# Batched matrix-product trace: last row tile loaded in other pieces, row 15 shared between TensorE and VectorE

## The chip, the cores and the metric

The kernel runs on one core of a Trainium2 chip. The metric is the device time of one execution in microseconds (us); each figure is a median of several runs. Before the change the time was 709.94 us (3 runs).

## The reference

```python
def reference(a, b):                        # a, b: (8, 2176, 2176) float32
    prod = np.matmul(a, b)
    return np.diagonal(prod, axis1=1, axis2=2).sum(axis=-1)
```

The trace of a product needs no product: it is the sum over all i, k of a[i, k] * b[k, i]. So the kernel transposes a, multiplies it element by element with b, and adds everything up. All 303 MB of the inputs must be read once.

## The kernel before

For each batch the rows of `a` are loaded as bf16, transposed by TensorE and copied into the tile `at`. The rows of `b` then come in groups of 128 (a "row tile", 17 in a batch, numbered 0 to 16). There are two ways to use one:

- VectorE: one fused multiply-and-reduce of a row tile with its part of `at`. It shows as CUSTOM_DVE_ANT_1, followed by a short read of the accumulator.
- TensorE: the row tile is cut into blocks of 128 columns. Each block is a matmul of a block of `at` with a block of `b`, added into one 128 x 128 tile, `trace_ps`. Only the diagonal of it is wanted; VectorE takes it at the end with a multiply-and-reduce against the identity (the "diagonal reduction" below, CUSTOM_DVE_ANT_0).

A row tile has five column groups: four of 512 columns (4 matmuls each) and a narrow one of 128 columns (1 matmul). In seven of the eight batches VectorE does all rows of `b`. In the last batch some go to TensorE, so that little is left to do when the last bytes arrive:

```python
PE_ROWS = (11, 12, 13, 15)
LAST_PIECES = [(0, 2), (2, 3), (3, 5)]      # column groups of row 16: three DMAs
...
def multiply_on_pe(at, row, v, g0, g1, parts=ROWS):
    for g in range(g0, g1):
        x, y = words_at(at, v, g, g + 1), words_of(row, g, g + 1)
        if g == n_wide:                      # the narrow group: weights from the row
            pe_work.append((row[:, g * WIDE:N], x.rearrange("q r x -> q x r")))
        else:                                # weights from at
            pe_work.extend((x[:, r, :], y[:, r, :]) for r in range(parts))
...
# row 16, the last one
multiply_on_pe(at, row, v0, 0, 1)
late.append((words_at(at, v0, 1, 2), words_of(row, 1, 2)))
half = ROWS // 2
for g in range(2, n_wide):
    multiply_on_pe(at, row, v0, g, g + 1, parts=half)
    late.append((words_at(at, v0, g, g + 1)[:, half:, :], words_of(row, g, g + 1)[:, half:, :]))
multiply_on_pe(at, row, v0, n_wide, len(a_groups))
...
for n, (x, y) in enumerate(pe_work):         # all TensorE work, in this order
    nc.tensor.matmul(trace_ps, x, y, start=(n == 0), stop=(n == len(pe_work) - 1))
...
for x, y in late:                            # VectorE's last reductions, in this order
    multiply_reduce(x, y, late_acc[:, cols:cols + 1]); cols += 1
multiply_reduce(tiles[f32], trace_ps, late_acc[:, cols:cols + 1], out=tiles["diagonal"])
# then: ones x late_acc on TensorE, a short sum on VectorE, the output DMA
```

Of the kernel before, what the change touches and what calls it, by code (L numbers as in the profile page):

```python
# [10 lines left out]
def row_groups(p, rows):  # L11

    groups, at = [], 0
    for m in rows:
        groups.append((at, m))
        at += m * p
    return groups
# [3 lines left out]
def kernel(  # L21
# [20 lines left out]
    a_groups = row_groups(P, even)  # L42
# [2 lines left out]

    UNEVEN = ((0, 80), (80, 119), (119, P))

    PE_ROWS = (11, 12, 13, 15)

    LAST_PIECES = [(0, 2), (2, 3), (3, 5)]  # L50

    const = ctx.enter_context(tc.tile_pool(name="const", bufs=1))
    at_pool = ctx.enter_context(tc.tile_pool(name="at_pool", bufs=1))
# [6 lines left out]
    def joined(groups):  # L60

        loads = []
        for start, m in groups:
            if m == ROWS and loads and loads[-1][1:] == (ROWS, 1):
                loads[-1] = (loads[-1][0], ROWS, DOUBLE)
            else:
                loads.append((start, m, 1))
        return loads
# [3 lines left out]
    def in_order():  # L72

        return tc.issue_after(loaded[-1].ins) if loaded else nullcontext()

    def fetch(t, src, start, m, count, parts=((0, P),)):

        rows = src[start:start + P * m * count, :].rearrange("(g p r) k -> p g r k", g=count, r=m)
        part = t.rearrange("p (g r) k -> p g r k", r=m)
        for lo, hi in parts:  # L80
            with in_order():
                issued = nc.gpsimd.dma_start(out=part[lo:hi], in_=rows[lo:hi])  # L82
            loaded.append(issued)
        return [(start + g * P * m, m, t[:, g * m:(g + 1) * m, :]) for g in range(count)], issued

    def load(src, start, m, count, parts=((0, P),)):
        if m == 1:
            t = single.tile([P, 1, N], bf16, tag="single")
        else:
            t = stage.tile([P, DOUBLE * ROWS, N], bf16, tag="stage")  # L90
        return fetch(t[:, 0:count * m, :], src, start, m, count, parts)

    def load_first(src, start):

        words = stage.tile([P, DOUBLE * ROWS, N], bf16, tag="stage")
        plain = words.bitcast(f32).rearrange("p r k -> p (r k)")[:, :N]
        half = N // 2
        t = single.tile([P, 1, N], bf16, tag="single")
        nc.sync.dma_start(out=plain, in_=src[start:start + P, :])
        nc.scalar.copy(out=t[:, 0, :half], in_=plain[:, :half])  # L100
        nc.vector.tensor_copy(out=t[:, 0, half:], in_=plain[:, half:])  # L101
        return [(start, 1, t)]
# [3 lines left out]
    def constants():  # L106
        identity32 = const.tile([P, P], f32, tag="identity32")
        make_identity(nc, identity32)
        identity16 = const.tile([P, P], bf16, tag="identity16")
        make_identity(nc, identity16)  # L110
        ones = const.tile([P, 1], f32, tag="ones")
        nc.vector.memset(ones, 1.0)
        sums = const.tile([P, BATCH], f32, tag="sums")
        late = const.tile([P, 2 * NT], f32, tag="late")
        diagonal = const.tile([P, P], bf16, tag="diagonal")
        result = const.tile([P, BATCH], f32, tag="result")
        tiles.update(ones=ones, sums=sums, late=late, result=result, diagonal=diagonal)
        tiles[f32], tiles[bf16] = identity32, identity16
# [12 lines left out]
    def multiply_reduce(x, y, acc, out=None):  # L131

        nc.vector.tensor_tensor_reduce(  # L133
            out=x if out is None else out, in0=x, in1=y, scale=1.0, scalar=0.0,
            op0=MUL, op1=ADD, accum_out=acc,
        )
# [4 lines left out]
    n_wide = NT // ROWS  # L141
# [58 lines left out]
    def words_of(row, g0, g1):  # L200

        return row[:, g0 * WIDE:min(g1 * WIDE, N)].rearrange("q (x r) -> q r x", r=ROWS)

    def words_at(at, v, g0, g1):
        return at[:, :, v, g0 * P:min(g1 * P, WORDS)]
# [3 lines left out]
# [4 lines that stand above are left out]
            if g == n_wide:  # L213
                pe_work.append((row[:, g * WIDE:N], x.rearrange("q r x -> q x r")))
            else:
                pe_work.extend((x[:, r, :], y[:, r, :]) for r in range(parts))

    late = []
    ahead = None
    for bi in range(BATCH):  # L220
        last = bi == BATCH - 1
        b_groups = row_groups(P, fine if last else even)


        at = at_pool.tile([P, ROWS, NT, WORDS], bf16, tag="at")
        loads = joined(a_groups)
        if bi == 0:
            loads = loads[-1:] + loads[:-1]
        for start, m, count in loads:
            if not tiles:  # L230
                groups = load_first(a[bi], start)
                ahead, issued = load(a[bi], *loads[1])
                with tc.issue_after(issued.ins):
                    constants()
            elif ahead is not None:
                groups, ahead = ahead, None
            else:
                groups, _ = load(a[bi], start, m, count)
            for start, m, a_t in groups:
                last_transpose = transpose_group(at, a_t, start, m, b_groups)  # L240


        copies_end = last_copy
        acc = tiles["late"] if last else acc_pool.tile([P, NT], f32, tag="acc")
        cols = 0

        def on_dve(v0, rows):

            nonlocal cols
            m = rows.shape[1]  # L250
            with tc.issue_after(copies_end.ins):
                multiply_reduce(
                    at[:, :, v0:v0 + m, :].rearrange("q r v x -> q r (v x)"),
                    rows.rearrange("q s (x r) -> q r (s x)", r=ROWS),
                    acc[:, cols:cols + 1],
                )
            cols += 1

        if not last:
            for start, m, count in joined(b_groups):  # L260
                parts = UNEVEN if bi == BATCH // 2 and m == 1 else ((0, P),)
                groups, _ = load(b[bi], start, m, count, parts)
                for start, m, b_t in groups:
                    on_dve(start // P, b_t)
            nc.vector.reduce_sum(  # L265
                out=tiles["sums"][:, bi:bi + 1], in_=acc[:, :cols], axis=mybir.AxisListType.X
            )
            continue

        used = DOUBLE * ROWS  # L270
        for start, m in b_groups:
            v0 = start // P
            if start < N - P:

                if used + m > DOUBLE * ROWS or m < ROWS and used == ROWS:
                    shared = stage.tile([P, DOUBLE * ROWS, N], bf16, tag="stage")
                    used = 0
                (group,), _ = fetch(shared[:, used:used + m, :], b[bi], start, m, 1)
                used += m
                b_t = group[2]  # L280
                mine = [s for s in range(m) if v0 + s not in PE_ROWS]
                if mine:
                    on_dve(v0 + mine[0], b_t[:, mine[0]:mine[-1] + 1, :])
                for s in range(m):
                    if s not in mine:
                        multiply_on_pe(at, b_t[:, s, :], v0 + s, 0, len(a_groups))
                continue
            b_t = single.tile([P, 1, N], bf16, tag="single")
            row = b_t[:, 0, :]
            for g0, g1 in LAST_PIECES:  # L290
                lo, hi = g0 * WIDE, min(g1 * WIDE, N)
                with in_order():
                    loaded.append(nc.gpsimd.dma_start(  # L293
                        out=row[:, lo:hi], in_=b[bi, start:start + P, lo:hi]
                    ))
            multiply_on_pe(at, row, v0, 0, 1)
            late.append((words_at(at, v0, 1, 2), words_of(row, 1, 2)))
            half = ROWS // 2
            for g in range(2, n_wide):
                multiply_on_pe(at, row, v0, g, g + 1, parts=half)  # L300
                late.append((words_at(at, v0, g, g + 1)[:, half:, :], words_of(row, g, g + 1)[:, half:, :]))
            multiply_on_pe(at, row, v0, n_wide, len(a_groups))


    trace_ps = psum_small.tile([P, P], f32, tag="trace")
# [57 lines left out]
```

## Time and profile before

| what | value | how to read it |
|---|---|---|
| time | 709.94 us | median of 3 runs |
| span of the profile | 707.9 us | the recorded part of one run |
| busiest engine | VectorE, 56% | no compute engine is the bound over the whole |
| DMA engines | 90% busy or more in 39 of 40 slices | the loads are the bound until they end |
| row 15 of the last batch lets TensorE start | 701.58 us | all that follows is "the tail" |
| diagonal reduction starts | 705.12 us | 3.54 us after that |

In the timeline a line has the start, the duration, the engine (PE is TensorE, PEld its weight loads, DVE is VectorE), the line of the kernel, the operation, output<-inputs, the shape and the count. In brackets it has the idle time before, and what ended it. `shared` holds the rows of the last batch up to row 15, `b_t` is row 16. The prediction shows the lines of the kernel before.

### The profile page before, as it was taken

How to read it: one execution, taken by the hardware profiler on the slowest of the kernel's cores; microseconds unless marked ns; L12 is line 12 of the kernel's file. 1: busy time of each engine (PE TensorE's matmuls, PEld its weight loads, DVE VectorE, ACT ScalarE, POOL GpSimd, SP SyncE). 2: the span in 40 equal slices, each digit the busy share in tenths (PEclk: the TensorE clock that was granted, in tenths of full speed). 3: DMA queues.
4: the chain of work that ended last, by engine and by line, in shares of the span. 5: the costliest groups of instructions: out<-in, count | busy, mean ns of one | idle time of the engine just before them, and what ended most of it. 6: DMA issues, size and time to landing. Idle time of an engine off the chain costs nothing.

```text
span 707.9 us, 3257 instructions
## 1 busy us (share of the span) xinstructions
PE 194.4 (27%) x1322; PEld 180.3 (25%) x1322; DVE 399.6 (56%) x200; ACT 196.5 (28%) x211; POOL 36.0 (5%) x63
## 2 busy tenths in 40 slices
PE   1542005420055100651005500056000670005605
PEld 0432005420054100551005500056000660005605
DVE  0222995138942389424893338933489334883396
ACT  2443005430064200642006510066100660006700
POOL 1000000000010000000001000000000000000100
PEclk9977557675577755776557765577655775557855
DMA  9999999999999999999999999999999999999997
GB/s 220 220 219 213 210 222 220 216 209 216 224 219 209 219 218 220 211 217 219 217 212 216 219 219 212 217 219 216 214 215 219 217 214 215 219 218 216 212 215 153
DMA packets 11681, 152.28 MB, mean 215 GB/s; under 512 B 914, under 2 KB 1170, under 8 KB 3346
## 3 DMA queue, kind: packets, MB, share of 16 engines
q0 software_dynamic: 11520, 150.97, 100.3%
q1 hardware_dynamic: 146, 1.11, 0.4%
q8 instruction: 10, 0.16, 0.1%
q14 instruction: 5, 0.04, 0.0%
HBM read 303.04 MB, written 0.00 MB: 428 GB/s over the span
## 4 chain that ended last, share of the span: by engine, by line
DMA 58%; DVE 24%; another core or an unknown queue 8%; issue 6%; PE 2%; ACT 1%; POOL 1%; DVEq 0%; POOLq 0%
DMA t<-in_b_dram 41%; DVE at L133 23%; DMA t<-in_a_dram 13%; DMA shared<-in_b_dram 4%; PE ps L167 1%; ACT at L128 1%; DVE at L126 1%; PE trace_ps L308 0%; POOL t L82 0%; PE ps L188 0%; POOL shared L82 0%; DVE acc L133 0%; POOL identity masks.py:199 0%; DVEq L133 0%
## 5 line engine op out<-in xcount | busy, mean ns | idle before, releaser
L128 ACT COPY at<-ps 128x1024 bf16<-128x1024 bf16 x208 | 194.1, 1051 | 471.4 <-PE ps L167 471.4
L133 DVE CUSTOM_DVE_ANT_1 at<-at,t 128x8704 bf16<-128x8704 bf16 (+1 forms) x35 | 273.6, 7862 | 81.2 <-DMA t<-in_b_dram 81.2
L167 PE MATMUL ps<-identity,t 128*128 128x128 f32 x1071 | 174.2, 328 | 481.8 <-DMA t<-in_a_dram 471.1
L167 PEld LDWEIGHTS ps<-identity,t 128*128 128x128 f32 x1071 | 162.0, 213 | 491.1 <-issue 463.0
L126 DVE COPY at<-ps 128x1024 bf16<-128x1024 bf16 (+2 forms) x104 | 94.2, 909 | 214.8 <-PE ps L167 197.7
L82 POOL DMA_DIRECT2D t<-in_a_dram x23 | 15.3, 669 | 344.3 <-DVE acc L133 199.9
L133 DVE CUSTOM_DVE_ANT_1 at<-at,shared 128x8704 bf16<-128x8704 bf16 (+2 forms) x4 | 27.8, 6955 | 1.9 <-DMA shared<-in_b_dram 1.9
L82 POOL DMA_DIRECT2D t<-in_b_dram x23 | 14.8, 646 | 237.7 <-PE ps L188 118.5
L188 PE MATMUL ps<-identity,t 128*128 128x128 bf16 x170 | 16.4, 219 | 5.1 <-DVE at L126 4.7
L188 PEld LDWEIGHTS <-t 128*128 128x128 bf16 x170 | 13.0, 100 | 8.5 <-issue 8.2
L308 PEld LDWEIGHTS <-at 128*128 128x128 bf16 x72 | 8.3, 124 | 24.7 <-issue 24.5
L308 PE MATMUL trace_ps<-shared,at 128*128 128x128 bf16 x64 | 8.1, 294 | 23.9 <-DMA shared<-in_b_dram 23.9
L82 POOL DMA_DIRECT2D shared<-in_b_dram x6 | 3.2, 537 | 55.1 <-PE ps L188 35.8
L101 DVE CAST t<-words 128x1088 bf16<-128x1088 f32 x1 | 0.7, 727 | 4.8 <-DMA words<-in_a_dram 4.8
L133 DVE DVE_READ_ACCUMULATOR2_ANT acc<- 128x1 f32 x35 | 2.9, 82 | 0.0
L133 DVE CUSTOM_DVE_ANT_1 at<-at,b_t 128x256 bf16<-128x256 bf16 (+1 forms) x3 | 1.5, 515 | 1.7 <-DMA b_t<-in_b_dram 1.7
L100 ACT CAST t<-words 128x1088 bf16<-128x1088 f32 x1 | 1.1, 1099 | 3.7 <-DMA words<-in_a_dram 3.7
L293 POOL DMA_DIRECT2D b_t<-in_b_dram x3 | 1.6, 567 | 0.0
L308 PE MATMUL trace_ps<-at,shared 128*128 128x128 bf16 x4 | 1.6, 396 | 0.0
L100 ACT ACT_TABLE_LOAD x1 | 1.3, 1283 | 0.7 <-PEq L347 0.7
L265 DVE TENSOR_REDUCE sums<-acc 128x1 f32<-128x5 f32 x7 | 1.1, 158 | 0.2
L308 PE MATMUL trace_ps<-b_t,at 128*128 128x128 bf16 x8 | 1.1, 296 | 0.0
(18 smaller groups left out, 4.3 us busy)
## 6 DMA issues: line engine op xcount, KB each, us to landing
t<-in_a_dram POOLq DMA_DIRECT2D x16, 4352.0 KB, 45.6
t<-in_b_dram POOLq DMA_DIRECT2D x14, 4352.0 KB, 52.2
shared<-in_b_dram POOLq DMA_DIRECT2D x3, 2176.0 KB, 43.0
t<-in_a_dram POOLq DMA_DIRECT2D x7, 544.0 KB, 47.4
t<-in_b_dram POOLq DMA_DIRECT2D x6, 544.0 KB, 54.8
words<-in_a_dram SPq DMA_DIRECT2D x1, 1088.0 KB, 4.9
shared<-in_b_dram POOLq DMA_DIRECT2D x1, 1088.0 KB, 26.1
shared<-in_b_dram POOLq DMA_DIRECT2D x2, 544.0 KB, 29.3
```

The source lines that it names most:

```text
L82: issued = nc.gpsimd.dma_start(out=part[lo:hi], in_=rows[lo:hi])
L100: nc.scalar.copy(out=t[:, 0, :half], in_=plain[:, :half])
L101: nc.vector.tensor_copy(out=t[:, 0, half:], in_=plain[:, half:])
L126: last_copy = nc.vector.tensor_copy(out=dst, in_=src)
L128: nc.scalar.copy(out=dst, in_=src)
L133: nc.vector.tensor_tensor_reduce(out=x if out is None else out, in0=x, in1=y, scale=1.0, scalar=0.0, op0=MUL, op1=ADD, accum_out=acc,)
L167: nc.tensor.transpose(ps[:, n * m + r, :], words[:, r, c0:c0 + step * (P - 1) + 1:step], tiles[f32],)
L188: last_transpose = nc.tensor.transpose(ps16[:, n, r, :], a_t[:, r, c0:c0 + P], tiles[bf16],)
L265: nc.vector.reduce_sum(out=tiles["sums"][:, bi:bi + 1], in_=acc[:, :cols], axis=mybir.AxisListType.X)
L293: loaded.append(nc.gpsimd.dma_start(out=row[:, lo:hi], in_=b[bi, start:start + P, lo:hi]))
L308: nc.tensor.matmul(trace_ps, x, y, start=(n == 0), stop=(n == len(pe_work) - 1),)
```

## The change

The intent is to shorten what TensorE has still to do after the last load. Row 15 is no longer all TensorE's: VectorE gets 1152 of its 2176 columns. The last row comes from the right, the wide piece with the narrow group first, so that two short matmuls and a short reduction are left for the last piece.

```diff
-    PE_ROWS = (11, 12, 13, 15)
-    LAST_PIECES = [(0, 2), (2, 3), (3, 5)]
+    PE_ROWS = (11, 12, 13)
+    SHARED_ROW = 15
+    LAST_PIECES = [(2, 5), (1, 2), (0, 1)]
 ...
+                if v0 == SHARED_ROW:
+                    row = b_t[:, 0, :]
+                    multiply_on_pe(at, row, v0, 0, 2)
+                    late.append((words_at(at, v0, 2, 5), words_of(row, 2, 5)))
+                    continue
 ...
-            multiply_on_pe(at, row, v0, 0, 1)
-            late.append((words_at(at, v0, 1, 2), words_of(row, 1, 2)))
+            multiply_on_pe(at, row, v0, n_wide - 1, len(a_groups))
+            late.append((words_at(at, v0, 2, n_wide - 1), words_of(row, 2, n_wide - 1)))
             half = ROWS // 2
-            for g in range(2, n_wide):
+            for g in (1, 0):
                 multiply_on_pe(at, row, v0, g, g + 1, parts=half)
                 late.append((words_at(at, v0, g, g + 1)[:, half:, :], words_of(row, g, g + 1)[:, half:, :]))
-            multiply_on_pe(at, row, v0, n_wide, len(a_groups))
```

## The prediction

> **What bounds the kernel now.** I read the page of the profile first, then the chain that ended last, then the timeline of its last microseconds. On the page, the engines' shares and the slices give the answer for most of the span:
>
> ```profile
> PE 194.4 (27%) x1322; PEld 180.3 (25%) x1322; DVE 399.6 (56%) x200; ACT 196.5 (28%) x211; POOL 36.0 (5%) x63
> ...
> DMA  9999999999999999999999999999999999999997
> ...
> HBM read 303.04 MB, written 0.00 MB: 428 GB/s over the span
> ```
>
> No engine is busy for more than 56%, while the 16 DMA engines are full in 39 of 40 slices; only the last slice shows a 7. So the loads bind until they end, and the change moves none of their bytes. What it can change is what happens around and after the last loads. The chain says how the end hangs together:
>
> ```profile
> 671.22 30.32 DMA shared<-in_b_dram
> 701.54 0.04 issue
> 701.58 3.39 PE trace_ps L308 x26
> 704.97 0.03 issue
> ...
> 705.12 0.29 DVE diagonal L133
> ```
>
> Row 15 of the last batch (a "shared" tile) lands at 701.54. From there on the chain is not DMA but 26 matmuls in a row: 17 of row 15 and 9 of the last row (b_t). Then VectorE reduces the diagonal of the TensorE product, and the final sum and the output follow. The timeline shows both engines in that stretch:
>
> ```profile
> 701.58 2.01 PE L308 MATMUL trace_ps<-shared,at 128*128 128x128 bf16 x16 [0.91 <-DMA shared<-in_b_dram]
> ...
> 702.82 0.69 DVE L133 CUSTOM_DVE_ANT_1 at<-at,b_t 128x512 bf16<-128x512 bf16 x1 [1.34 <-DMA b_t<-in_b_dram]
> ...
> 703.47 0.43 DVE L133 CUSTOM_DVE_ANT_1 at<-at,b_t 128x256 bf16<-128x256 bf16 x1
> 703.63 1.11 PE L308 MATMUL trace_ps<-b_t,at 128*128 128x128 bf16 x8
> ...
> 704.26 0.43 DVE L133 CUSTOM_DVE_ANT_1 at<-at,b_t 128x256 bf16<-128x256 bf16 x1 [0.36 <-DMA b_t<-in_b_dram]
> 704.45 0.13 PEld L308 LDWEIGHTS <-b_t 128*128 128x128 bf16 x1
> 704.56 0.40 PE L308 MATMUL trace_ps<-at,b_t 128*128 128x128 bf16 x1
> 704.62 0.09 DVE L133 DVE_READ_ACCUMULATOR2_ANT late<- 128x1 f32 x1
> 705.12 0.29 DVE L133 CUSTOM_DVE_ANT_0 diagonal<-identity,trace_ps 128x128 bf16<-128x128 f32 x1 [0.42 <-PE trace_ps L308]
> ```
>
> Three readings. TensorE begins the last row at 703.63, some 0.8 us after its first piece let VectorE go (702.82): it is behind by the work of row 15. VectorE in the same time waits: 1.34 us for the first piece and 0.36 us for the last. The last piece released VectorE at 704.26, so by the same 0.04 us of lag that row 15 shows (701.54 to 701.58) it landed at about 704.22; a count over 704.3 to 708.0 shows no DMA share at all. TensorE reaches that piece (the seventh of the nine matmuls) only at 703.63 + 6 x 0.116 = 704.33, so it never waits for it. The bound after the loads is thus the tail of a backlog, and a short one: the lag is about 0.1 us.
>
> **What the Trainium skill says.** "TensorE: Matmul & The Clock Gate", section "Single matmul latency", gives (219+N)/1.2 ns for the cold clock: for N = 128 that is 289 ns. The granted clock is 0.50 from 680 us on, and the matmuls take 292 to 297 ns: it agrees. Its section "LDWEIGHTS" gives P/1.2, 107 ns; this trace has 123 to 127 ns, and the pitch of the pairs is (704.56 - 703.63)/8 = 0.116 us. I use the trace's pitch. "VectorE: DVE Perf Modes", section "The TRN2 errata", tells of a fixed cost per instruction beside the elements, some 150 cycles measured at 0.96 GHz. Here 512 elements take 693 ns and 256 take 426 ns, so 1.04 ns each and 0.16 us fixed, which is about 154 cycles: it agrees. "DMA: Bandwidth & Descriptors", section "Queues, rings and completion order", has each DMA engine consume its descriptors in ring order, without a guarantee that writes complete in it. The releases at 702.82 and 704.26 follow the order of issue, and I assume that for the new pieces.
>
> **The change, part by part.** The bytes are the same, as are the number of DMAs (three for the last row) and their queue, so I keep 704.22 for the last landing. The last row takes 704.22 - 701.54 = 2.68 us for 2176 columns, or 1.23 ns a column. As a check, the old first piece of 1024 columns gives 702.80 by this, and VectorE was let go at 702.82. The new landings (estimates): 1152 columns at 702.96, 512 more at 703.59, the last 512 at 704.22.
>
> TensorE. Of row 15 it keeps column groups 0 and 1, 2 x 4 = 8 matmuls of 17; 9 go. They start at 701.58 and end 8 x 0.116 later, at 702.51, so TensorE is idle when the first piece lands. That piece is 5 matmuls (one group of 4 and the narrow one of 128 columns): from 703.00 on, issued by 703.58. The second is 2 matmuls, from 703.63 to 703.86. The third is 2 matmuls, from 704.26: the second starts at 704.38 and takes 0.29, so the product is done at 704.67. Before it was done at 704.97. The 0.30 us has three parts: the backlog of 0.07 to 0.1 (704.33 against 704.26); one matmul fewer in the last piece, 0.116; and a last matmul of 0.29 in place of 0.40, as the narrow one, whose weights come from the row itself, is no longer last.
>
> VectorE. It gains one reduction of 1152 elements: 0.16 + 1152 x 1.04 ns = 1.36 us. It was free from 701.48 (the accumulator read after row 14), so this runs from 701.58 to 702.94, to about 703.0 with the read of its sum: within the wait of 1.34 us shown above. Then 512 elements of the first piece, 703.0 to 703.65 (the old one took 0.65 to the next start); 256 of the second, to 704.05; 256 of the third from 704.26, with the read done at 704.71 as before. No part of the 1.36 us reaches the end, with some 0.2 us to spare before the third.
>
> After that: the diagonal started 0.15 us after the product (704.97 to 705.12). So it starts at 704.82 in place of 705.12. The final sum has 9 columns for 8, which is nothing. **Sum:** 0.30 us off the path that sets the end, from 709.94 to 709.64, or 0.04%.
>
> **The rivals.**
> - VectorE becomes the bound. If the first piece lands later than its share, or the 1152 elements take up to 0.2 us longer, the three short reductions queue up and its last read could be at 704.9 or so; the diagonal then starts at 704.95 and the gain is 0.15 us: 709.8. For it: VectorE loses nearly all of its waiting. Against it: the slack above.
> - The reductions write their product over their input in the transposed tile. If the order of accesses were kept for the whole row, VectorE would wait for TensorE's 8 matmuls of row 15: start at 702.8, then 1.4 + 0.65 + 0.4 + 0.4 gives 705.65, 0.8 us later than my start of the diagonal: 710.4. Against it: before, VectorE works on the last row at 702.82, ahead of TensorE's reads of that row at 703.63, so no such wait is there.
> - The loads decide, and the tail drowns. The runs before differ by 0.32 us (709.71 to 710.03), as much as the whole gain. A load stream that is 0.05% different, 0.35 us of 704 us, gives anything from 709.3 to 710.0. Against a greater shift: the sizes of descriptors hardly change (the pieces were 1024, 512 and 640 columns), and a slightly shorter last piece cannot bring its landing forward while the bytes before it are the same.
> - Nothing is gained as the last landing alone sets the end: 709.9. Against it: the product ends 0.75 us after the landing, more than the 0.40 us that two matmuls need after it.
>
> **Range and chances.** The path gives 709.64; VectorE's possible lateness adds up to 0.15 on one side, so I say 709.65. The spread of runs and of the stream, 0.35 us either way, joined with the uncertainty of the tail, gives 709.2 to 710.2 for 8 in 10. For 2% the time would have to move 14 us, and everything after row 15 landed is only 6.4 us: I give "same" 0.99.
>
> **What would show it.** In the changed profile: TensorE idle before the first and the last piece of b_t, released by its DMA; a reduction of 1152 elements of about 1.36 us beginning within 0.1 us of TensorE's first matmul of row 15; the chain going through the DMA of b_t rather than of row 15; the product done some 0.45 us after the last landing instead of 0.75. I would be wrong if the last landing itself moved by more than 0.3 us relative to the start, if VectorE's last short reduction began later than the last landing plus 0.1 us, or if the 1152 elements waited for TensorE.

## The result, and the profile after

The changed kernel took 709.57 us (median of 6 runs, 709.44 to 709.82), the kernel before 709.84 us beside it (6 runs, 709.64 to 710.10): 0.27 us less. The ratio is 0.9996 with a 95% interval of 0.9983 to 1.0009, so "same".

The page of the changed kernel, its engine shares, DMA row of the slices and bytes read:

```profile
PE 194.1 (27%) x1313; PEld 179.9 (25%) x1313; DVE 401.0 (57%) x202; ACT 196.4 (28%) x211; POOL 36.0 (5%) x63
...
DMA  9999999999999999999999999999999999999997
...
HBM read 303.04 MB, written 0.00 MB: 428 GB/s over the span
```

TensorE has 9 matmuls fewer and VectorE one reduction more (two instructions, with the read of its sum), 1.4 us of it. The bytes, the rate and the DMA row are the same, so any difference has to be looked for in the tail. The chain that ended last, in order of time (start, duration, what):

```profile
672.96 31.44 DMA b_t<-in_b_dram
704.39 0.02 issue
704.42 0.43 DVE at L135
...
704.87 0.02 DVEq L135
704.89 0.10 issue
704.99 0.29 DVE diagonal L135
```

Before, the chain left the loads at row 15 and ran through 26 matmuls. Now it stays on the loads until the last piece of row 16 (704.39), and after that it has one short reduction. (`DVEq` is VectorE's sequencer, here waiting for a semaphore, the signal by which one engine tells another that it is done; it will matter below.) The timeline of the same stretch:

```profile
701.73 1.36 DVE L135 CUSTOM_DVE_ANT_1 at<-at,shared 128x1152 bf16<-128x1152 bf16 x1
701.75 1.09 PE L314 MATMUL trace_ps<-shared,at 128*128 128x128 bf16 x8 [0.91 <-DMA shared<-in_b_dram]
...
703.13 0.69 DVE L135 CUSTOM_DVE_ANT_1 at<-at,b_t 128x512 bf16<-128x512 bf16 x1
703.15 0.62 PE L314 MATMUL trace_ps<-b_t,at 128*128 128x128 bf16 x4 [0.32 <-DMA b_t<-in_b_dram]
...
703.59 0.40 PE L314 MATMUL trace_ps<-at,b_t 128*128 128x128 bf16 x1
...
703.81 0.41 PE L314 MATMUL trace_ps<-b_t,at 128*128 128x128 bf16 x2
...
704.42 0.43 DVE L135 CUSTOM_DVE_ANT_1 at<-at,b_t 128x256 bf16<-128x256 bf16 x1 [0.21 <-DMA b_t<-in_b_dram]
704.44 0.39 PE L314 MATMUL trace_ps<-b_t,at 128*128 128x128 bf16 x2 [0.22 <-DMA b_t<-in_b_dram]
...
704.77 0.08 DVE L135 DVE_READ_ACCUMULATOR2_ANT late<- 128x1 f32 x1
704.99 0.29 DVE L135 CUSTOM_DVE_ANT_0 diagonal<-identity,trace_ps 128x128 bf16<-128x128 f32 x1
```

TensorE now waits 0.32 us for the first piece and 0.22 us for the last: it has no backlog, that is, no matmuls of earlier pieces left when a piece lands. VectorE begins row 15 together with TensorE, and still waits 0.21 us for the last piece. In this run TensorE's row 15 began 0.17 us later than in the profile of before (701.75 against 701.58), so the absolute times must not be compared. From TensorE's first matmul of row 15 to the diagonal reduction it is 704.99 - 701.75 = 3.24 us, against 3.54 before.

This interval is the yardstick for the experiments. It is sound because what lies after it does not change. The time of the profiled run less the start of its diagonal reduction is 709.70 - 705.12 = 4.58 us before and 709.59 - 704.99 = 4.60 after; in all ten profiles it lies between 4.56 and 4.60. So a profiled run's time is the start of row 15, plus the interval, plus 4.58 us to within 0.02.

### The profile page after: what moved, and what is told of

Read it like the earlier page. It is cut to its first block, busy times and chain, and to the rows that moved or that the text cites. A ratio compares the mean times of both kernels' runs of the same rounds, so it can differ in the third digit from the quotient of the medians.

```text
span 707.8 us, 3241 instructions
## 1 busy us (share of the span) xinstructions
PE 194.1 (27%) x1313; PEld 179.9 (25%) x1313; DVE 401.0 (57%) x202; ACT 196.4 (28%) x211; POOL 36.0 (5%) x63
## 4 chain that ended last, share of the span: by engine, by line
DMA 58%; DVE 24%; another core or an unknown queue 8%; issue 6%; PE 2%; ACT 1%; POOL 1%; DVEq 0%; POOLq 0%
DMA t<-in_b_dram 41%; DVE at L135 24%; DMA t<-in_a_dram 13%; DMA b_t<-in_b_dram 4%; PE ps L169 2%; ACT at L130 1%; DVE at L128 1%; POOL t L84 0%; POOL shared L84 0%; PE ps L190 0%; POOL b_t L300 0%; DVE acc L135 0%; POOL identity masks.py:199 0%; DVEq L135 0%
## 5 line engine op out<-in xcount | busy, mean ns | idle before, releaser
L135 DVE CUSTOM_DVE_ANT_1 at<-at,shared 128x8704 bf16<-128x8704 bf16 (+3 forms) x5 | 29.2, 5838 | 2.0 <-DMA shared<-in_b_dram 1.9
```

The costliest lines, as they stand in the source:

```text
L135: nc.vector.tensor_tensor_reduce(out=x if out is None else out, in0=x, in1=y, scale=1.0, scalar=0.0, op0=MUL, op1=ADD, accum_out=acc,)
```

## The experiments

All ran in two sets of five rounds. Within a set the kernels ran on the same chip and shared the runs of the kernel before: 709.75 us (9 runs, 709.62 to 710.14) in the first set, 709.83 us (9 runs, 709.69 to 710.23) in the second. Every result was correct. The 95% intervals of the ratios all contain 1 (they are some 0.0013 wide on each side, 0.9 us). Start and interval are those of the profiled run.

| kernel | row 15 starts | interval, us | median, us | ratio |
|---|---|---|---|---|
| before | 701.58 | 3.54 | 709.84 | |
| changed | 701.75 | 3.24 | 709.57 | 0.9996 |
| after_again (set 1) | 701.70 | 3.25 | 709.41 | 0.9995 |
| shared_only (1) | 701.70 | 3.47 | 709.75 | 0.9999 |
| pieces_only (1) | 701.70 | 3.54 | 709.70 | 0.9998 |
| row15_vector (1) | 701.74 | 3.66 | 709.86 | 1.0001 |
| after_third (set 2) | 701.58 | 3.24 | 709.42 | 0.9996 |
| share_12 (2) | 701.67 | 3.25 | 709.70 | 1.0 |
| last_256 (2) | 701.61 | 3.14 | 709.40 | 0.9995 |
| four_pieces (2) | 701.46 | 3.08 | 709.25 | 0.9994 |

(row15_vector has no TensorE work on row 15; its interval counts from VectorE's start, which in the other kernels that share the row lies 0.02 us before TensorE's.)

### after_again and after_third: is the difference real?

No edit.

> The changed kernel once more, with more rounds. My theory (the backlog of TensorE after row 15 landed is taken away, the last piece needs two short matmuls): 0.30 us less than the kernel before, so a ratio of 0.9996, and from TensorE's first matmul of row 15 to the start of the diagonal reduction 3.24 us in place of 3.54 us. The rival that the difference is only noise of the load stream: a median difference under 0.1 us.

> The changed kernel beside these on the same chip, as their yardstick: 0.3 us less than the kernel before, first matmul of row 15 to diagonal 3.24 us.

The medians are 0.34 and 0.41 us below those of before, and the intervals are 3.25 and 3.24 us. In the first set all five runs (709.38 to 709.55) lie below the lowest of the nine of before (709.62); in the second the ranges touch (709.28 to 709.77 against 709.69 to 710.23). The gain is there each time, of about the size of the interval's 0.30 us. That it is only noise of the loads is unlikely after this, although the loads do vary as much: row 15 started anywhere between 701.46 and 701.75 us in the ten profiles. But medians alone can't settle its size: below, share_12 has the same interval as the changed kernel and a median 0.28 us higher. The size rests on the interval.

### shared_only: only row 15 shared

```diff
 # the kernel before, with:
-    PE_ROWS = (11, 12, 13, 15)
+    PE_ROWS = (11, 12, 13)
+    SHARED_ROW = 15          # and the branch for it, as in the change
```

> Only the first half of the change: row 15 shared, the last row in the old pieces of 1024, 512 and 640 columns in the old order. My theory: TensorE is free when the last piece lands but has three matmuls left, the last of them the slow narrow one of 0.40 us; product done 0.63 us after it starts on that piece, so first matmul of row 15 to diagonal about 3.46 us, 0.08 us less than before. Rival (the backlog alone was the cost, the pieces are worth nothing): 3.24 us, 0.30 us less.

The end of the timeline:

```profile
704.40 0.39 PE L315 MATMUL trace_ps<-b_t,at 128*128 128x128 bf16 x2 [0.40 <-DMA b_t<-in_b_dram]
...
704.61 0.40 PE L315 MATMUL trace_ps<-at,b_t 128*128 128x128 bf16 x1
...
705.17 0.29 DVE L135 CUSTOM_DVE_ANT_0 diagonal<-identity,trace_ps 128x128 bf16<-128x128 f32 x1 [0.35 <-PE trace_ps L315]
```

The backlog is gone (TensorE waits 0.40 us for the last piece), yet the interval is 3.47 us, 0.07 less than before. The rest is the third matmul after the last landing, the narrow one of 0.40 us: from the start on the last piece to the end of the product it is 0.61 us here (704.40 to 705.01) and 0.39 us in the changed kernel (704.44 to 704.83). The rival, that the backlog alone was the cost, falls. The median of the runs shows no gain at all; 0.07 us is below what they resolve.

### pieces_only: only the new pieces

```diff
 # the changed kernel, with:
-    PE_ROWS = (11, 12, 13)
-    SHARED_ROW = 15          # and without the branch for it
+    PE_ROWS = (11, 12, 13, 15)
```

> Only the second half: the new pieces from the right, row 15 wholly on TensorE. My theory: TensorE's 26 matmuls still run in one piece from the landing of row 15 and never wait; the last matmul is short (0.29 for 0.40 us) but the narrow one now delays the matmul after it by 0.1 us in the middle, so first matmul of row 15 to diagonal stays about 3.53 us, a gain of 0.0 to 0.1 us. Rival (the pieces alone bring the gain): 3.24 us.

```profile
703.76 0.64 PE L307 MATMUL trace_ps<-b_t,at 128*128 128x128 bf16 x4
...
704.23 0.40 PE L307 MATMUL trace_ps<-at,b_t 128*128 128x128 bf16 x1
...
704.44 0.64 PE L307 MATMUL trace_ps<-b_t,at 128*128 128x128 bf16 x4
...
705.24 0.29 DVE L133 CUSTOM_DVE_ANT_0 diagonal<-identity,trace_ps 128x128 bf16<-128x128 f32 x1 [0.42 <-PE trace_ps L307]
```

No idle time stands before any of these matmuls: TensorE works through all 26 from 701.70 on, and the interval is 3.54 us, as before. The last matmul is indeed short. But the narrow one, now in the middle, lets the next matmul start only 0.21 us after itself (704.23 to 704.44) instead of 0.116 us, so on an engine with a backlog its cost merely moves. The two halves of the change give 0.07 and 0.00 us alone and 0.30 us together. The new pieces pay only where TensorE waits for them, and the freed TensorE pays only if little is left for the last piece.

### row15_vector: all of row 15 on VectorE

```diff
 # the changed kernel, with:
-                    multiply_on_pe(at, row, v0, 0, 2)
-                    late.append((words_at(at, v0, 2, 5), words_of(row, 2, 5)))
+                    late.append((words_at(at, v0, 0, 5), words_of(row, 0, 5)))
```

> The change driven too far: row 15 wholly on VectorE (2176 elements), TensorE none of it. My theory: VectorE's reduction takes 2.43 us instead of 1.36, its slack before the last piece is only about 0.2 us, so the three short reductions queue up and the diagonal starts about 3.9 us after row 15 landed, 0.7 us later than with the change and 0.4 us later than before: about 710.2 us. Rival (VectorE's time is hidden anyway by the loads): same as the change, 709.6 us.

```profile
701.74 2.42 DVE L135 CUSTOM_DVE_ANT_1 at<-at,shared 128x2176 bf16<-128x2176 bf16 x1
...
704.09 0.69 DVE L135 CUSTOM_DVE_ANT_1 at<-at,b_t 128x512 bf16<-128x512 bf16 x1
704.71 0.42 DVE L135 CUSTOM_DVE_ANT_1 at<-at,b_t 128x256 bf16<-128x256 bf16 x1
705.05 0.42 DVE L135 CUSTOM_DVE_ANT_1 at<-at,b_t 128x256 bf16<-128x256 bf16 x1
...
705.40 0.28 DVE L135 CUSTOM_DVE_ANT_0 diagonal<-identity,trace_ps 128x128 bf16<-128x128 f32 x1
```

The direction was right: VectorE becomes the bound, its reductions queue up, and the kernel is slower than the changed one of the same set (after_again) by 0.41 us in the interval and 0.45 us in the median. The size was missed: I expected 3.9 us and 710.2 us, and it was 3.66 us and 709.86 us. The reason is in the starts. Reductions that need not wait follow each other after 2.35, 0.62, 0.34 and 0.35 us, 3.66 us in all. The expected 2.43 us with the prediction's steps of 0.65, 0.4 and 0.4 us gives the 3.9 us. The next reduction starts before the recorded end of the one in front: 704.09 against 701.74 + 2.42 = 704.16.

### share_12: the cut of row 15 elsewhere

```diff
 # the changed kernel, with:
-                    multiply_on_pe(at, row, v0, 0, 2)
-                    late.append((words_at(at, v0, 2, 5), words_of(row, 2, 5)))
+                    multiply_on_pe(at, row, v0, 0, 3)
+                    late.append((words_at(at, v0, 3, 5), words_of(row, 3, 5)))
```

> Row 15 split the other way: TensorE 12 matmuls of it (three column groups), VectorE 640 elements instead of 1152. My theory: both engines are free before the last piece in either split, so where the row is cut is not critical: first matmul of row 15 to diagonal 3.24 us as with the change, 709.5 us. Rival (TensorE's backlog scales with its share of row 15): 12 matmuls end at 1.40 us, later than the first piece at 1.42 by nothing, but if the narrow matmul adds its 0.1 us, some backlog stays and the diagonal starts at 3.3 us or later.

The interval is 3.25 us, as with the change: TensorE takes its first matmul of row 16 at 703.07, 0.02 us after VectorE was released by the same piece, and waits 0.22 us for the last piece. So by the trace the interval is the same with the row cut after 8 and after 12 matmuls. The time did not follow: 709.70 us (709.50 to 709.90) is 0.28 us above the changed kernel beside it, where I had expected 709.5. The profiled run is the fastest of the five; the other four have no trace, so where their time went stays open. The part of the theory about the runs' time is not confirmed.

### four_pieces and last_256: who holds the diagonal reduction?

The chain of the changed kernel says that the diagonal reduction followed VectorE's own last reduction, which ended at 704.42 + 0.43 = 704.85. TensorE's product ended at 704.44 + 0.39 = 704.83, almost the same. The two readings ask for different remedies, so I made two kernels in which TensorE has nothing to do for the last piece.

```diff
 # four_pieces: the changed kernel, with:
-    LAST_PIECES = [(2, 5), (1, 2), (0, 1)]
+    LAST_PIECES = [(2, 5), (1, 2), (0.5, 1), (0, 0.5)]   # 1152, 512, 256, 256 columns
 ...
-            half = ROWS // 2
-            for g in (1, 0):
-                multiply_on_pe(at, row, v0, g, g + 1, parts=half)
-                late.append((words_at(at, v0, g, g + 1)[:, half:, :], words_of(row, g, g + 1)[:, half:, :]))
+            multiply_on_pe(at, row, v0, 1, 2)
+            for c in (P // 2, 0):
+                late.append((words_at(at, v0, 0, 1)[:, :, c:c + P // 2], words_of(row, 0, 1)[:, :, c:c + P // 2]))
 # last_256: the same, with
+    LAST_PIECES = [(2, 5), (0.5, 2), (0, 0.5)]           # 1152, 768, 256 columns
```

> The change, with the last row in pieces of 1152, 512, 256 and 256 columns: TensorE takes all four matmuls of the second piece and nothing of the last two, VectorE the last two (256 elements each). My theory: in the changed kernel the diagonal reduction is held by TensorE's product (0.16 us after it), not by VectorE's last short reduction, though the chain names the latter. Here the product is done some 0.7 us after the second piece landed, before VectorE has read its last sum, so the diagonal follows that reduction without a gap: VectorE 256 elements from about 2.40 to 2.75 and 2.75 to 3.09 us after row 15's start, diagonal at about 3.05 to 3.1 us in place of 3.24, 0.15 to 0.2 us faster than the change. Rival (the diagonal waits for VectorE's own last reduction, as the chain has it, with 0.14 us to it): diagonal at 3.2 us or later, no gain. Another rival: the smaller pieces land later, by 0.1 us or more, and eat the gain.

> The change, with pieces of 1152, 768 and 256 columns: TensorE takes four matmuls of the 768 and nothing of the last piece; VectorE 256 elements of each of the last two. My theory: the piece of 768 lands about 2.35 us after row 15, so TensorE's four matmuls end at 3.05 and the diagonal starts at about 3.2 us: within 0.1 us of the change, product still the holder. Rival (VectorE's last reduction holds): VectorE's last starts at 2.74 and ends at 3.1, diagonal at 3.2 to 3.25, hardly to be told apart here; the gap between the last read of a sum and the diagonal tells.

The end of the timeline of four_pieces, then of last_256:

```profile
703.55 0.64 PE L313 MATMUL trace_ps<-b_t,at 128*128 128x128 bf16 x4
703.85 0.42 DVE L135 CUSTOM_DVE_ANT_1 at<-at,b_t 128x256 bf16<-128x256 bf16 x1 [0.28 <-DMA b_t<-in_b_dram]
...
704.20 0.42 DVE L135 CUSTOM_DVE_ANT_1 at<-at,b_t 128x256 bf16<-128x256 bf16 x1
704.54 0.08 DVE L135 DVE_READ_ACCUMULATOR2_ANT late<- 128x1 f32 x1
704.54 0.28 DVE L135 CUSTOM_DVE_ANT_0 diagonal<-identity,trace_ps 128x128 bf16<-128x128 f32 x1
```

```profile
703.98 0.62 PE L313 MATMUL trace_ps<-b_t,at 128*128 128x128 bf16 x4
...
704.65 0.08 DVE L135 DVE_READ_ACCUMULATOR2_ANT late<- 128x1 f32 x1
704.75 0.29 DVE L135 CUSTOM_DVE_ANT_0 diagonal<-identity,trace_ps 128x128 bf16<-128x128 f32 x1
```

From VectorE's last read of a sum to the diagonal reduction it is 0.22 us in the changed kernel (704.77 to 704.99), 0.10 in last_256 and 0.00 in four_pieces, where the product had been done since 704.19. From the end of the product it is 0.16 us in the changed kernel and 0.15 in last_256 (704.60 to 704.75), as in the kernel before (704.97 to 705.12). So in the changed kernel the product held the diagonal reduction, and the chain put the wait down to the wrong one of two ends that lie 0.02 us apart. The rival falls. The packed trace has a more direct witness, which I had overlooked: the `DVEq` line just before the diagonal reduction (704.87 in the changed kernel) is a wait for the semaphore that TensorE's last matmul raises. In all ten profiles it begins 0.04 us after the end of the product. It stands 0.12 us before the diagonal reduction in the eight profiles in which the product holds it, but 0.31 us before it in four_pieces and 0.50 in row15_vector, where VectorE's own reductions come last.

Both kernels also confirm the sizes: 3.08 us for four_pieces (expected 3.05 to 3.1) and 3.14 for last_256 (expected about 3.2, within 0.1 us of the change). The last piece of four_pieces landed 2.75 us after row 15, in the changed kernel 2.69 (from the landings in the packed traces). It came 0.06 us later, then, but still in time: at 704.16, and VectorE came to it at 704.20 without a wait. With 709.25 us, 0.17 us below the changed kernel beside it and 0.58 us below the kernel before, four_pieces has the lowest median of all kernels here. Its runs (709.12 to 709.66) overlap with those of the changed kernel (709.28 to 709.77), so that it beats the change is shown by the interval of one profile, and by the runs only in the median.

## Why the prediction was right

- **What bounds the kernel.** Right. The DMA engines were 90% busy or more in 39 of 40 slices in both kernels. A profiled run's time has three parts: the start of row 15 moved by 0.17 us, as it does between two profiles of the changed kernel alone (701.58 and 701.75); the interval fell by 0.30 us; and what follows stayed (4.58 and 4.60 us).
- **TensorE.** Right. It became idle before the first and the last piece (0.32 and 0.22 us); the product was done 704.83 - 704.39 = 0.44 us after the last landing, where I had said 0.45. One pitch was wrong: I gave all matmuls 0.116 us to the next start, but after the narrow one it is 0.22 (703.59 to 703.81). It cost nothing, as the second piece landed only at 703.76.
- **The sum of 0.30 us.** The interval went from 3.54 to 3.24 us, and the medians by 0.27, 0.34 and 0.41 us. The three terms of the sum (backlog, one matmul fewer, a shorter last one) hold only in that order. shared_only measured the first as 0.07 us. The other two, 0.23 us together where I had 0.116 and 0.11, exist only once the backlog is gone: pieces_only measured 0.00 us for them by themselves. How the 0.23 us divide between them no run shows.
- **VectorE.** Right: 1.36 us for the 1152 elements, begun 0.02 us before TensorE's first matmul, and 0.21 us of waiting left before the last piece, where I had said 0.2. What I made of VectorE's lateness in the rivals was somewhat too dark: row15_vector showed that queued reductions follow each other faster than I had added.
- **Landings.** The share of the bytes was a good guide. With row 15 0.17 us later, the first piece should have landed at 703.13, the second at 703.76 and the last at 704.39. The landings in the packed trace are 703.11, 703.76 and 704.40, in the order of issue, as I had assumed.
- **The rivals.** VectorE did not become the bound. No wait for TensorE's reads of row 15 appeared: VectorE started row 15 first. The noise of the loads is as large as the gain, as the rival had it, but repeated runs show a gain through it. That the last landing alone sets the end falls too: the landing stayed where it was, 2.70 and 2.69 us after row 15, and the interval fell by 0.30 us.
- **The range.** All six runs lie in 709.2 to 710.2, the median 0.08 us below the predicted 709.65. This says little: the range also holds 709.84 us, the kernel before beside them, so no gain at all would have fallen into it. Part of the closeness is luck as well: I started from 709.94 us, 0.10 us above what the kernel before had with more runs. The test of the mechanism is the interval.
- **Readings.** Two were too narrow: over the whole product the usual matmuls take 272 to 297 ns (I wrote 292 to 297) and the weight loads 98 to 127 ns (I wrote 123 to 127). Nothing in the sum rests on them.

## What to carry to other kernels

Where the loads bind a kernel to its end, as here, look first at what is left to do after the last bytes. Look for the engine that comes to the last piece late, and for the number and kind of instructions it has for that piece; taking away one without the other gave at most 0.07 of 0.30 us here. Where two engines end within hundredths of a microsecond, don't trust the chain on which of them held the next step: compare the gap after each over several kernels (the constant one points to the holder), or find which engine's semaphore the step waited for. Where two runs' loads differ by as much as the effect, measure from an event at the start of the tail and not from the start of the run.

## What the Trainium skill lacked or had wrong

- "TensorE: Matmul & The Clock Gate", section "Single matmul latency": its cold formula, 289 ns for 128 columns, fits the usual matmuls (median 294 ns, 272 to 297, at a granted clock of 0.50; the profile models the ends of matmuls), but not the narrow one, which takes its weights from the row and its moving operand from `at` in steps: 395 ns, and 0.22 us until the next matmul starts instead of 0.116. Whether the stepped operand is the cause was not tested.
- The same page, section "LDWEIGHTS": 128/1.2 = 107 ns; most of the weight loads of this product took 122 to 127 ns.
- "Perfetto Trace Analysis", section "Identifying Dependency Chains": it sends the reader to the semaphores of an instruction and to the extra EventSemaphore instructions before one that waits for several engines, which is the way that settles it here (the `DVEq` wait above). It lacks a warning for two candidates that end close together, where a chain can name the wrong one. Here the ends were 704.83 (product, the true holder) and 704.85 us (the one that the chain named), with 0.15 to 0.16 us from the product to the step in the kernels that it held.
